# Weight sums of a block product made in DRAM by accumulating transfers, and one down projection moved to block products

## The chip, the cores and the metric

The kernel runs on one core of a Trainium2 chip. TensorE (PE) multiplies, VectorE (DVE), ScalarE (ACT) and GpSimd (POOL) work elementwise, SyncE (SP) only issues transfers. Each engine has its own instruction stream and works through it in order; engines wait for one another by semaphores. Transfers that SP issues are seen in the profile under SPq; POOL can issue transfers too.

The metric is the device time in microseconds of one execution. Three runs of the kernel before took 2127.66, 2130.86 and 2133.08 us.

## The reference

One decoder layer on 2048 tokens of width 1024, all in float32:

```python
xn = rms_norm(h, mix_norm_w)
proj = xn @ w_in                                   # 1024 x 3072
q, f_logit, i_v, g, lru_x, lru_gate = split(proj)
mixed = concat([hgrn2_mix(q, f_logit, i_v, g), rglru_mix(lru_x, lru_gate)])
h = h + mixed @ w_out                              # 1024 x 1024
hn = rms_norm(h, ffn_norm_w)
gate, up = split(hn @ w_gate_up)                   # 1024 x 5632, 2816 each
h = h + (silu(gate) * up) @ w_down                 # 2816 x 1024
return rms_norm(h, final_norm_w)
```

`hgrn2_mix` is a gated linear recurrence over 4 heads, `rglru_mix` a short convolution with a gated scan over 512 channels.

## The kernel before

**Halves.** The 2048 tokens are worked in two halves of 1024. The program runs the mixers of the first half, the mixers of the second, then the FFN (gate/up, then down) of the first half, then the FFN of the second.

**Precision.** A float32 operand is split into a high part, rounded for the fast matmul, and a low part, the rest (`split`: a cast on ACT at L207 and a subtraction on DVE at L208, for the mixers' weights L163 and L164). A product is three matmuls: high by high, high by low, low by high.

**Mixers.** A loop over eight strips of features and two chunks of 512 tokens (`s`, `c`), 16 turns for each half, multiplies the normalized input with `w_in` (L234 to L236) and runs the two recurrences on ACT and DVE. The weights come as a stream `ws` of 512 KB pieces (SP, L161) into three raw buffers. POOL does three small things a turn: `hist` (L389) keeps the end of a chunk for the convolution, `hst` (L427) the end of a scan, and `oss` (L379) takes the power -1/2 of a head's mean square, which DVE's L380 then multiplies with.

**Gate/up.** The products of the FFN are made in blocks of 2 x 2 by seven products instead of eight (Winograd's form of Strassen's method). A "quad" is one such block product: 22 for each half, 44 in all, each of 7 products of 12 matmuls (4 slices of the depth, 3 matmuls each, L614). It needs seven weight operands: three blocks as they are, and four sums s1 to s4 of blocks. `Sums.load` fetches two transfers of 512 KB a quad, `Sums.make` makes the sums on DVE (L498, tile `s`) and splits each operand (tiles `wgu`). Four PSUM banks a quad (`quad_a`, `quad_e`, `quad_f`, `quad_g`) take the products; ACT copies two of them out (`e`, L651 and L654), DVE adds the others (`u`, `e`).

**Down.** `store` writes the gated activations: for the column pairs worked in blocks their seven operands (`ao_p`, float32), for the others as they are. `Group` is a set of up to four of the 11 pairs of columns: its four weight blocks are loaded (`wdax`, `wdbx`, `wday`, `wdby`), the sums are made from them on DVE, and seven products follow (`down_quads`, L885: for four pairs 48 matmuls a product, for three pairs 36). The second half uses three groups: 4, 4 and 3 pairs. The first half uses two groups of 4 pairs in blocks; its last three pairs, six columns, are multiplied plainly by `down_plain` (L752 to L754, 48 matmuls a column, 24 for each of the two chunks). `residual_load`, `square` and `finish` add the residual stream, take the squares and write the output.

**Order.** The program is written with `bops`, `later`, `extra` and `steps`, lists of small pieces of work that the loops hand out one at a time; on top of that, a scheduler decides the order of the instructions on each engine. Buffers come from pools with a fixed number of slots (16 of 128 x 512 in "pg", 9 for split weights in "w"); a load waits until its slot is free. SP and POOL work through their queues in order, and each of them waits for an earlier transfer when it comes to the ninth outstanding one.

Of the kernel before, what the change touches and what calls it, by code (L numbers as in the profile page):

```python
# [13 lines left out]
P = 128  # L14
# [21 lines left out]
def hybrid_layer(ctx: ExitStack, tc: tile.TileContext, x, x_t, norm_w, cols, w_in, gate_w, w_out, w_gu, w_down, out):  # L36
# [117 lines left out]
    class Stream:  # L154
# [3 lines left out]
        def emit(self, i):  # L158
            src, nm = self.specs[i]
            raw = rawt("raw_" + nm)  # L160
            nc.sync.dma_start(out=raw, in_=src)  # L161
            hi, lo = wslot("whi_" + nm), wslot("wlo_" + nm)
            nc.scalar.copy(out=hi, in_=raw)  # L163
            v.tensor_tensor(out=lo, in0=raw, in1=f(hi), op=ALU.subtract)  # L164
            self.made[i] = (hi, lo)
# [338 lines left out]
    def acts(src, nm, direct):  # L504
        ops = {}
        held = []

        def put(name, k, p):
            split([ops[name][s][:, k, :] for s in range(2)], p)

        pages = {}

        def open_(names):
            for name in names:
                ops[name] = [block(f"act_{LET[name]}{s}_{nm}") for s in range(2)]


        def early(k):
            if k == 0:
                open_(("p1", "p5"))  # L520
            b11, b12 = (xin(f"{t}{k}_{nm}") for t in ("b11e_", "b12e_"))
            for p, c in ((b11, 0), (b12, 1)):
                nc.sync.dma_start(out=p, in_=src[0][k, :, c * CW : (c + 1) * CW])
            put("p1", k, b11)
            tt_(b12, b12, b11, SUB_)
            put("p5", k, b12)

        def load(k):
            if k == 0:
                open_(("p1", "p5", "p6", "p7", "p2", "p3", "p4") if direct else ("p6", "p7", "p2"))  # L530
            b11, b12 = (xin(f"{t}{k}_{nm}") for t in ("b11_", "b12_"))
            b21, b22 = ((late if direct else page)(f"{t}{k}_{nm}") for t in ("b21_", "b22_"))
            for p, n, c in ((b11, 0, 0), (b12, 0, 1), (b22, 1, 1), (b21, 1, 0)):
                nc.sync.dma_start(out=p, in_=src[n][k, :, c * CW : (c + 1) * CW])
            pages[k] = b11, b12, b21, b22

        def one(k):
            b11, b12, b21, b22 = pages[k]
            if direct:
                put("p1", k, b11)  # L540
            tt_(b11, b12, b11, SUB_)
            if direct:
                put("p5", k, b11)

        def two(k):
            b11, b12, b21, b22 = pages[k]
            tt_(b11, b22, b11, SUB_)
            tt_(b12, b22, b12, SUB_)
            put("p2", k, b21)
            put("p6", k, b11)  # L550
            tt_(b21, b21, b11, SUB_)
            put("p7", k, b12)
            if direct:
                put("p3", k, b22)
                put("p4", k, b21)
            held.append((b22, b21))

        def rest(i):
            name = ("p3", "p4")[i]
            ops[name] = [block(f"act_{LET[name]}{s}_{nm}") for s in range(2)]  # L560
            for k in range(4):
                put(name, k, held[k][i])
# [5 lines left out]
        if direct:  # L568
            return ops, steps, []
        return ops, [[lambda k=k: early(k) for k in range(4)], steps], [lambda: rest(0), lambda: rest(1)]  # L570

    ORDER = ("p1", "p5", "p6", "p7", "p2", "p3", "p4")


    class Sums:
        def __init__(self, src, nm):
            self.src, self.nm, self.op, self.raw, self.done = src, nm, {}, [None, None], set()

        def load(self, i):
            r = rawt(f"raw{i}_{self.nm}", (P, 2, CW))  # L580
            nc.sync.dma_start(out=r, in_=self.src[:, :, i * CW : (i + 1) * CW].rearrange("u p k -> p u k"))
            self.raw[i] = r

        def make(self, i):
            (a11, a21), (a12, a22) = ([r[:, u, :] for u in range(2)] if r is not None else (None, None) for r in self.raw)
            nm, name = self.nm, ORDER[i]
            if name == "p1":
                x = a11
            elif name == "p5":
                self.s1 = x = late("s1" + nm)  # L590
                tt_(x, a21, a22, ADD)
            elif name == "p6":
                self.s2 = x = late("s2" + nm)
                tt_(x, self.s1, a11, SUB_)
            elif name == "p7":
                x = late("s3" + nm)
                tt_(x, a11, a21, SUB_)
            elif name == "p2":
                x = a12
            elif name == "p3":  # L600
                x = late("s4" + nm)
                tt_(x, a12, self.s2, SUB_)
            else:
                x = a22
            w = wslot(f"wgu_{LET[name]}_{nm}", (P, 2, CW))
            split([w[:, s, :] for s in range(2)], x)
            self.op[name] = w

    def product(ps, w, b, first):
        for k in range(4):  # L610
            ks = slice(k * P, (k + 1) * P)
            hi, lo = b[0][:, k, :], b[1][:, k, :]
            for n, (s, x) in enumerate(((0, hi), (1, hi), (0, lo))):
                nc.tensor.matmul(  # L614
                    ps, lhsT=w[:, s, ks], rhs=x, start=first and k + n == 0, stop=k == 3 and n == 2, skip_group_check=not first
# [6 lines left out]
    def sums(q):  # L622
        if q < len(quads) and q not in made:
            half, j, m = quads[q]
            f0 = m * NF + 2 * j
            made[q] = Sums(w_gu[f0 : f0 + 2], f"{half}_{j}_{m}")
        return made.get(q)

    def sums_start(q):
        s = sums(q)  # L630
        s.load(0)
        s.load(1)

    def ffn_up(half, bops, between=()):
        between = list(between)
        q0 = half * 2 * NPAIR
# [535 lines left out]
```

## Time and profile before

| | |
|---|---|
| median of three runs | 2130.86 us (2127.66 to 2133.08) |
| the profiled execution, first to last instruction | 2131.1 us |
| the same by the list of cores, with the granted TensorE clock | 2131.1 us, 0.997 |
| PE busy | 2101.2 us, 99% |
| DVE busy | 1493.1 us, 70% |
| ACT busy | 1010.2 us, 47% |
| POOL busy | 82.2 us, 4% |
| transfers, mean over the span | 123 GB/s |
| first mixers' loop, first to last matmul of its kind | 62.6 to 291.3 us |
| gate/up of the first half begins | 849.5 us |
| last matmul of the plain columns | 1494.9 us |
| last matmul of the second half's gate/up | 1914.0 us |

The profiled execution is first to last instruction 0.2 us above the median of the runs, so a difference worked out on the trace is used on the median as it is. In the profile a line such as `L614 PE MATMUL quad_a<-act_a,wgu_a 128*128 128x512 f32 x528 | 127.5, 389 | 0.0` gives the line of the program, the engine and operation, output and inputs, shape, count, busy microseconds, mean nanoseconds of one, and the idle time ahead. Matmuls overlap one another, so 389 ns is how long one lasts and not how far apart they come: 528 of them are busy 127.5 us.

### The profile page before, as it was taken

What the parts mean: (1) busy time and instruction counts of PE and PEld (TensorE: products, weight loads), DVE (VectorE), ACT (ScalarE), POOL (GpSimd) and SP (SyncE); (2) the same over time, 40 slices, a digit from 0 to 9 for tenths busy, and PEclk for the clock granted to TensorE, in tenths of its full rate; (3) what the DMA queues carried; (4) which work ended last, traced back from release to release, by engine and by line L of the source; (5) the groups of instructions that cost most, each with busy time, mean ns of one, the idle gap of its engine ahead of it and who ended that gap; (6) DMA issues with size and microseconds to landing.
All of it is one profiled execution on the core that took longest, in us unless ns stands there. A gap on an engine that the chain in (4) does not pass through costs nothing.

```text
span 2131.1 us, 26161 instructions
## 1 busy us (share of the span) xinstructions
PE 2101.2 (99%) x9704; PEld 1735.7 (81%) x9704; DVE 1493.1 (70%) x2415; ACT 1010.2 (47%) x1647; POOL 82.2 (4%) x130
## 2 busy tenths in 40 slices
PE   8999999999999999999999999999999999999998
PEld 6887888888878888788888888888888888888887
DVE  6577664645776566877667669878867667669787
ACT  5577764535777644533333334335433333334333
POOL 2000001100000000000000000000000000000000
PEclk9999999999999999999999999999999999999999
DMA  6111104852111058433323257346423223257424
GB/s 216 61 40 40 40 20 160 282 162 69 31 39 40 20 174 260 156 112 99 106 93 129 89 187 253 109 136 205 143 94 119 95 90 123 94 206 252 156 88 143
DMA packets 138420, 262.84 MB, mean 123 GB/s; under 512 B 11186, under 2 KB 27570, under 8 KB 138292
## 3 DMA queue, kind: packets, MB, share of 16 engines
q1 hardware_dynamic: 138292, 261.17, 36.5%
q8 instruction: 76, 1.25, 0.2%
q14 instruction: 52, 0.43, 0.1%
HBM read 197.95 MB, written 63.18 MB: 123 GB/s over the span
## 4 chain that ended last, share of the span: by engine, by line
PE 83%; ACT 6%; DVE 5%; DMA 3%; issue 2%; SPq 0%; POOL 0%; DVEq 0%; POOLq 0%; ACTq 0%
PE quad_e L614 11%; PE quad_g L614 11%; PE quad_a L614 11%; PE pda L885 10%; PE pdb L885 6%; PE quad_f L614 5%; PE poh L246 2%; PE poh L247 2%; PE poh L248 2%; PE pb L236 2%; PE pb L234 2%; PE pb L235 2%; PE pa L234 1%; PE pa L235 1%; PE pg L248 1%
## 5 line engine op out<-in xcount | busy, mean ns | idle before, releaser
L614 PE MATMUL quad_f<-act_f,wgu_f 128*128 128x512 f32 x528 | 127.4, 389 | 1.8 <-DVE h L1050 1.7
L614 PE MATMUL quad_a<-act_a,wgu_a 128*128 128x512 f32 x528 | 127.5, 389 | 0.0
L614 PE MATMUL quad_g<-act_d,wgu_d 128*128 128x512 f32 x528 | 127.0, 389 | 0.2 <-DVE u L498 0.2
L614 PE MATMUL quad_g<-act_g,wgu_g 128*128 128x512 f32 x528 | 127.1, 390 | 0.0
L614 PE MATMUL quad_a<-act_b,wgu_b 128*128 128x512 f32 x528 | 127.1, 389 | 0.0
L614 PE MATMUL quad_e<-act_e,wgu_e 128*128 128x512 f32 x528 | 127.0, 389 | 0.0
L614 PE MATMUL quad_e<-act_c,wgu_c 128*128 128x512 f32 x528 | 126.9, 389 | 0.0
L614 PEld LDWEIGHTS quad_f<-act_f,wgu_f 128*128 128x128 f32 x528 | 99.0, 188 | 23.1 <-ACT act_g L207 2.1
L498 DVE TENSOR_TENSOR u<-u,quad_g 128x512 f32<-128x512 f32 x88 | 60.5, 687 | 80.9 <-PE quad_g L614 80.9
L614 PEld LDWEIGHTS quad_g<-act_d,wgu_d 128*128 128x128 f32 x528 | 99.0, 188 | 21.1 <-DVE u L498 0.6
L614 PEld LDWEIGHTS quad_e<-act_c,wgu_c 128*128 128x128 f32 x528 | 99.1, 188 | 20.6
L614 PEld LDWEIGHTS quad_g<-act_g,wgu_g 128*128 128x128 f32 x528 | 99.0, 188 | 20.8 <-DVE wgu_g L208 0.3
L614 PEld LDWEIGHTS quad_e<-act_e,wgu_e 128*128 128x128 f32 x528 | 99.0, 188 | 20.6
L614 PEld LDWEIGHTS quad_a<-act_b,wgu_b 128*128 128x128 f32 x528 | 99.0, 188 | 20.5
L614 PEld LDWEIGHTS quad_a<-act_a,wgu_a 128*128 128x128 f32 x528 | 98.9, 188 | 20.6 <-ACT act_c L207 0.2
L234 PE MATMUL pa<-xn,whi_in 128*128 128x512 f32 x256 | 101.7, 397 | 0.0
L236 PE MATMUL pb<-xn,whi_in 128*128 128x512 f32 x256 | 101.0, 395 | 0.0
L235 PE MATMUL pb<-xn,wlo_in 128*128 128x512 f32 x256 | 101.0, 394 | 0.0
L234 PE MATMUL pb<-xn,whi_in 128*128 128x512 f32 x256 | 100.9, 394 | 0.0
L235 PE MATMUL pa<-xn,wlo_in 128*128 128x512 f32 x256 | 100.6, 393 | 0.0
L236 PE MATMUL pa<-xn,whi_in 128*128 128x512 f32 x256 | 100.5, 393 | 0.0
L248 PE MATMUL poh<-whi_o,mx 128*128 128x512 f32 x256 | 99.9, 391 | 0.0
(331 smaller groups left out, 4940.9 us busy)
## 6 DMA issues: line engine op xcount, KB each, us to landing
raw<-in_w_gu SPq DMA_DIRECT2D x88, 512.0 KB, 3.8
raw_in<-in_w_in SPq DMA_DIRECT2D x48, 512.0 KB, 3.5
ao_p<-as SPq DMA_DIRECT2D x76, 256.0 KB, 2.6
raw_o<-in_w_out SPq DMA_DIRECT2D x32, 512.0 KB, 4.4
x<-in_x SPq DMA_DIRECT2D x32, 256.0 KB, 5.8
xrh<-in_x SPq DMA_DIRECT2D x32, 256.0 KB, 3.9
h<-h SPq DMA_DIRECT2D x32, 256.0 KB, 3.5
hn<-hths SPq DMA_DIRECT2D x32, 256.0 KB, 3.3
```

Of the source, the lines that this page charges most:

```text
L234: nc.tensor.matmul(ps, lhsT=whi[:, ks], rhs=hi, start=(k == 0), stop=False)
L235: nc.tensor.matmul(ps, lhsT=wlo[:, ks], rhs=hi, start=False, stop=False)
L236: nc.tensor.matmul(ps, lhsT=whi[:, ks], rhs=lo, start=False, stop=(k == KT - 1))
L246: nc.tensor.matmul(ps, lhsT=hi, rhs=whi[:, ks], start=(k == 0), stop=False)
L247: nc.tensor.matmul(ps, lhsT=hi, rhs=wlo[:, ks], start=False, stop=False)
L248: nc.tensor.matmul(ps, lhsT=lo, rhs=whi[:, ks], start=False, stop=(k == KT - 1))
L498: (e or v).tensor_tensor(out=out, in0=a, in1=b, op=op)
L614: nc.tensor.matmul(ps, lhsT=w[:, s, ks], rhs=x, start=first and k + n == 0, stop=k == 3 and n == 2, skip_group_check=not first)
L885: nc.tensor.matmul(ps, lhsT=x, rhs=y, start=first and q + n == 0, stop=q == gr.n - 1 and n == 2, skip_group_check=not first)
```

## The change

It lays the FFN weights out in DRAM by quadrants, makes the four sums of both weight matrices in DRAM, and works all of the first half's down projection in blocks.

- **Sums in DRAM.** `combine` makes them for a piece of two quads (or two column pairs of `w_down`), 17 pieces in all: step 0 is four copies of 512 KB, DRAM to DRAM, issued by SP behind the latest weight load of the mixers; steps 1, 2 and 3 are two, one and one accumulating transfers issued by POOL, each adding a block, or a sum made before, onto a copy. `combines(t)` hands them out in the mixers' loop, a new piece every one and a half turns and a step of a piece every two turns. 11 pieces belong to gate/up, 6 to down.
- **Gate/up.** A quad loads its seven operands ready, as 256 KB each (`Sums.load`), and splits them two at a time (128 x 1024). The form of the method is another one: the signs differ, three banks a quad instead of four, products in the order p1, p5, p6, p3, p7, p2, p4, three copies out of PSUM on ACT, and fewer DVE operations.
- **Store.** For the last three column pairs of either half the seven operands are split already here (`keep_`) and written as high and low parts, 14 transfers instead of seven.
- **Down.** Both halves use the groups of 4, 4 and 3 pairs. A group loads its weight operands ready (`wr`, L810). The group of three loads its activation operands already split, straight into slots of the "w" pool (`aop`, L831). The second half's activation operands are made in pieces during the first half's down (`extra`), and the output of the first half's first four tiles is written during the second half's gate/up.

```diff
-            nc.sync.dma_start(out=raw, in_=src)
+            self.last = nc.sync.dma_start(out=raw, in_=src)
...
+    def combine(w, sums_, p, step):
+        s1, s2, s3, s4 = (sums_[i][p] for i in range(4))
+        n = s1.shape[0]
+        a11, a12, a21, a22 = (w[i, p * PIECE : p * PIECE + n] for i in range(4))
+        if step == 0:
+            with tc.issue_after(ws.last.ins):
+                for s, a in ((s1, a21), (s3, a11), (s2, a11), (s4, a12)):
+                    nc.sync.dma_start(out=s, in_=a)
+        else:
+            for s, a in (((s1, a22), (s3, a21)), ((s2, s1),), ((s4, s2),))[step - 1]:
+                nc.gpsimd.dma_start(out=s, in_=a, accum_op=ADD, max_dma_last_dim=8192)
+
+    def combines(t):
+        for i, piece in enumerate(pieces):
+            step, odd = divmod(t - 3 * i // 2, 2)
+            if not odd and 0 <= step < 4:
+                combine(*piece, step)
...
         def load(self, i):
+            names = ORDER[2 * i : 2 * i + 2]
             r = rawt(f"raw{i}_{self.nm}", (P, 2, CW))
-            nc.sync.dma_start(out=r, in_=self.src[:, :, i * CW : (i + 1) * CW].rearrange("u p k -> p u k"))
+            for u, name in enumerate(names):
+                nc.sync.dma_start(out=r[:, u, :], in_=summed(w_gu, gu_s, name, self.q, 1)[0])
...
         def make(self, i):
-            elif name == "p5":
-                self.s1 = x = late("s1" + nm)
-                tt_(x, a21, a22, ADD)
-            elif name == "p6":
-                self.s2 = x = late("s2" + nm)
-                tt_(x, self.s1, a11, SUB_)
...
+            hi, lo = (wslot(f"wgu{'hl'[z]}{i}_{self.nm}", (P, 2, CW)) for z in range(2))
+            split((hi[:, 0:n, :], lo[:, 0:n, :]), self.raw.pop(i)[:, 0:n, :])
...
-            b1, b3, b2, b4 = (mk(f"quad_{i}_{nm}") for i in "aefg")
-            dst = dict(p1=b1, p5=b3, p6=b2, p7=b4, p2=b1, p3=b3, p4=b4)
+            ba, bb, bc_ = (mk(f"quad_{i}_{nm}") for i in "abc")
+            dst = dict(p1=ba, p5=bb, p6=ba, p3=bb, p7=ba, p2=bc_, p4=ba)
...
+        def keep_(name, p):
+            hl = [sb.tile([P, CW], F32R, tag="late", name=f"ah{z}_{name}_{half}_{j}", bufs=5) for z in range(2)]
+            split(hl, p, -1.0 if name == "p6" else None)
+            for z in range(2):
+                nc.sync.dma_start(out=as_d[half][name][z][j - SPLIT], in_=f(hl[z]))
...
         def fetch(self, i):
             name = DORDER[i]
+            t = block(f"wr_{LET[name]}_{self.nm}", F32)
+            for k, m in self.parts():
+                nc.sync.dma_start(out=t[:, k : k + m, :], in_=summed(w_down, dn_s, name, self.j0 + k, m).rearrange("g p t -> p g t"))
+            self.wraw[i] = t
+            if self.split:
+                return
...
         def make(self, i, part):
+                if self.split:
+                    for (k, m), t in zip(self.parts(), self.a[name]):
+                        j = self.j0 - SPLIT + k
+                        for z in range(2):
+                            nc.sync.dma_start(out=f(t[z])[:, 0:m, :], in_=as_d[self.half][name][z][j : j + m].rearrange("g p t -> p g t"))
...
+                combines(half * 16 + s * NC + c)
...
     for half in range(2):
-        ffn_up(half, bops[half], later if half == 0 else ())
-        hp = residual(half)
+        ffn_up(half, bops[half], later)
+        hp, later = residual(half), []
...
-            down_quads(0, ((0, 4), (4, 4)), hp, False)
-            bops[1], steps, last = acts(hn_d[1], "1", True)
...
-            for c in range(NC):
-                down_plain(0, c, range(16, NF), hp, extra, [lambda i=i: first(i) for i in range(7)] if c == 1 else ())
...
-            down_quads(1, ((0, 4), (4, 4), (8, 3)), hp, True)
+        down_quads(half, hp, extra, later)
```

In the rows below the line numbers of the program after are its own; a product of the block method that is L614 before is L636 after, and L885 is L875.

POOL in the first mixers' loop, from the first head's `oss` on. Before:

```order
L379 TENSOR_TENSOR oss_0_0_936<-oss_0_0_936,tinies 128x4
L389 COPY hist<-xp_1_1_1109 128x3
L379 TENSOR_TENSOR oss_0_1_1052<-oss_0_1_1052,tinies 128x4
L427 COPY hst<-t_1_0_1071 128x1
L427 COPY hst<-t_1_1_1171 128x1
L389 COPY hist<-xp_3_0_1485 128x3
L379 TENSOR_TENSOR oss_2_0_1418<-oss_2_0_1418,tinies 128x4
```

The same place after (`gus` are the gate/up sums; 8 and 10 are two pieces):

```order
L379 TENSOR_TENSOR oss_0_0_1028<-oss_0_0_1028,tinies 128x4
L596 DMA gus_6_114<-gus_6_103 64x2048
L596 DMA gus_6_136<-gus_6_114 64x2048
L389 COPY hist<-xp_1_1_1203 128x3
L379 TENSOR_TENSOR oss_0_1_1146<-oss_0_1_1146,tinies 128x4
L596 DMA gus_8_104<-in_w_gu 64x2048
L596 DMA gus_8_126<-in_w_gu 64x2048
L596 DMA gus_10_105<-in_w_gu 64x2048
L596 DMA gus_10_127<-in_w_gu 64x2048
L427 COPY hst<-t_1_0_1165 128x1
L596 DMA gus_8_115<-gus_8_104 64x2048
L596 DMA gus_10_116<-gus_10_105 64x2048
```

POOL's small operations now stand behind accumulating transfers, of which one that reads a sum (`gus_6_136<-gus_6_114`) follows the one that makes it.

SP in the same loop, after; before, the four weight loads stand there with nothing between them:

```order
L161 DMA raw_in_12_1480<-in_w_in 128x1024
L161 DMA raw_in_13_1486<-in_w_in 128x1024
L593 DMA gus_8_104<-in_w_gu 16x8192
L593 DMA gus_8_126<-in_w_gu 16x8192
L593 DMA gus_8_115<-in_w_gu 16x8192
L593 DMA gus_8_137<-in_w_gu 16x8192
L593 DMA gus_10_105<-in_w_gu 16x8192
L593 DMA gus_10_127<-in_w_gu 16x8192
L593 DMA gus_10_116<-in_w_gu 16x8192
L593 DMA gus_10_138<-in_w_gu 16x8192
L161 DMA raw_in_14_1727<-in_w_in 128x1024
L161 DMA raw_in_15_1733<-in_w_in 128x1024
```

Eight copies of 512 KB now lie between one pair of weight loads and the next.

SP in the group of three of the first half's down, after:

```order
L810 DMA wr_f_8_11826<-dns_8_154 128x2x512
L810 DMA wr_f_8_11826<-dns_10_155 128x512
L831 DMA aop_f_0_8_11864<-as_p_222 128x2x512
L831 DMA aop_f_0_8_11865<-as_p_223 128x2x512
L831 DMA aop_f_0_8_11866<-as_p_222 128x512
L831 DMA aop_f_0_8_11867<-as_p_223 128x512
L810 DMA wr_e_8_11889<-dns_8_148 128x2x512
L810 DMA wr_e_8_11889<-dns_10_149 128x512
```

Each product of that group has its weight operand fetched in two transfers and its split activation operand in four; before, this part of the program was plain columns with a load of 512 KB of weights and 256 KB of activations each.

More of the change, by code (lines that the diff above doesn't have):

```diff
@@ L524, in early @@
             put("p1", k, b11)
-            tt_(b12, b12, b11, SUB_)
+            tt_(b12, b11, b12, SUB_)
             put("p5", k, b12)
         def load(k):
[L529 to L534, printed above, removed]
@@ L564, in acts, with four @@
+        def four(f_):
+            return [lambda k=k: f_(k) for k in range(4)]
         steps = [lambda: load(0)]
@@ L567, in acts, with sum_tiles @@
             steps.append(lambda k=k: two(k))
[L568 to L572, printed above, removed]
+        return ops, [four(early), steps], [lambda: rest(0), lambda: rest(1)], [four(f_) for f_ in (early, mid, third, fourth, fifth)]
+    ORDER = ("p1", "p5", "p6", "p3", "p7", "p2", "p4")
+    PIECE = 2
+    NQ = 2 * NPAIR
+    def sum_tiles(n, nm):
+        return [
+            [dram.tile([min(PIECE, n - p), P, CW], F32, name=f"{nm}{i}_{p}") for p in range(0, n, PIECE)] for i in range(4)
+        ]
@@ L630, in sums_start @@
         s = sums(q)
-        s.load(0)
-        s.load(1)
+        for i in range(3):
+            s.load(i)
     def ffn_up(half, bops, between=()):
-        between = list(between)
-        q0 = half * 2 * NPAIR
-        for q in range(q0, q0 + 2 * NPAIR):
+        between, chores = list(between), []
+        q0 = half * NQ
+        for q in range(q0, q0 + NQ):
             _, j, m = quads[q]
             nm = f"{half}_{j}_{m}"
-            s, nxt, nn = sums(q), sums(q + 1), sums(q + 2)
+            s, nxt = sums(q), sums(q + 1)
@@ L691, in ffn_up @@
-                if nxt is not None and not end:
-                    nxt.make(i)
-                    nxt.done.add(i)
+                        sg21 = page("sg21" + nm)
+                        nc.scalar.activation(out=sg21, in_=ba, func=AF.Silu, scale=-1.0)
+                    else:
+                        v.scalar_tensor_tensor(out=sg21, in0=ba, scalar=-1.0, in1=sg21, op0=MUL, op1=MUL)
+                        chores = store(half, j, a11, a21, sg21, a22)
+                ahead(s, nxt, i, end)
@@ L859, in down_quads @@
         u2 = {}
-        groups[0].load()
         fetch(0)
@@ L898, in down_quads @@
                     tt_(h00, h00, ps, ADD)
-                    if end and last:
+                    if end:
                         square(half, tt, 0, h00)
```

367 lines of the change are left out of this document (165 added, 202 removed).

## Prediction

> **What bounds the kernel now.** I read the list of cores first (2131.1 us, clock 0.997: nothing throttled), then the page's engine line, then windows of the stages.
>
> ```profile
> core 0: 2131.1 us, clock 0.997
> PE 2101.2 (99%) x9704; PEld 1735.7 (81%) x9704; DVE 1493.1 (70%) x2415; ACT 1010.2 (47%) x1647; POOL 82.2 (4%) x130
> ```
>
> TensorE is idle for 30 us of the whole span. The windows say where (columns: stretch, its length, busy time and count of PE, weight loads, DVE, ACT, POOL, then clock, share of the DMA engines, GB/s):
>
> ```profile
> 160.00:213.00 53.00, 50.13 (x245) 41.45 (x244) 37.93 (x88) 40.86 (x66) 3.93 (x6) 0.97 0.12 40
> 852.00:905.00 53.00, 50.52 (x232) 40.02 (x231) 46.42 (x79) 31.31 (x65) 3.94 (x4) 1.00 0.47 154
> 905.00:1280.00 375.00, 375.00 (x1656) 310.52 (x1655) 256.03 (x379) 131.53 (x216) 0.00 (x0) 1.00 0.34 118
> 1276.00:1300.00 24.00, 24.00 (x108) 19.87 (x107) 24.00 (x23) 12.66 (x15) 0.00 (x0) 1.00 1.03 369
> 1500.00:1914.00 414.00, 414.00 (x1828) 342.80 (x1827) 289.68 (x434) 145.64 (x241) 1.74 (x2) 1.00 0.35 119
> 2090.00:2131.00 41.00, 33.61 (x149) 27.50 (x147) 32.51 (x56) 12.40 (x29) 4.84 (x8) 0.95 0.45 154
> ```
>
> From 905 us on PE is busy 375 of 375 and 414 of 414 us in the two gate/up stretches, and 24 of 24 even where DVE and the DMA engines are full. What is idle lies in the mixers (2.9 us in the stretch shown), at the start of gate/up (2.5 us) and at the tail (7.4 us). So in the FFN only the number of matmuls can shorten the time, as long as what feeds them stays ahead. The chain of waits gives the spacing of the matmuls:
>
> ```profile
> PE 83%; ACT 6%; DVE 5%; DMA 3%; issue 2%; SPq 0%; POOL 0%; DVEq 0%; POOLq 0%; ACTq 0%
> 1935.93 10.88 PE pdb L885 x48
> ```
>
> 10.88 / 48 = 0.2267 us for each.
>
> **Removed: 36 matmuls.** The plain columns are 288 matmuls on the path:
>
> ```profile
> L752 PE MATMUL pd<-whi_d,ad 128*128 128x512 f32 x96 | 36.6, 391 | 0.7 <-DVE hd L498 0.7
> L753 PE MATMUL pd<-wlo_d,ad 128*128 128x512 f32 x96 | 37.4, 389 | 0.0
> L754 PE MATMUL pd<-whi_d,ad 128*128 128x512 f32 x96 | 37.4, 389 | 0.0
> L885 PE MATMUL pda<-wd_a,aop_a 128*128 128x512 f32 x228 | 53.1, 389 | 0.0
> ```
>
> The 228 of a product are 4 groups of 48 and one of 36; the new group of three adds 36 to each of seven products, 252. All other matmuls stay. 288 x 0.2267 = 65.3 us become 252 x 0.2267 = 57.1 us: **-8.2 us**. The plain stage's wait of 0.7 us for `hd` goes with it: **-0.7 us**.
>
> **Removed: DVE work, worth nothing.** A quad made four sums, in groups such as
>
> ```profile
> L498 DVE TENSOR_TENSOR s<-raw,s 128x512 f32<-128x512 f32 x44 | 30.4, 691 | 1.2
> L164 DVE TENSOR_TENSOR wlo_in<-raw_in,whi_in 128x1024 fp32r<-128x1024 f32 x48 | 58.6, 1220 | 22.0 <-PE pv L248 7.1 <-PE pb L235 6.3 <-ACT whi_in L163 5.0
> ```
>
> 4 x 0.69 = 2.8 us a quad on DVE, about 120 us in 44 quads; splits of 128 x 1024 at 1.22 us instead of two at 0.69 save a little more. PE covers it all: DVE was busy 256 of 375 us and PE never idle. I book 0; the 2.5 us at the start of gate/up, where DVE is busiest, is the most that could come back.
>
> **Moved: banks in gate/up.** Three banks a quad are handed on more often. In the new order of the matmuls at least 22 lie between a bank's last matmul and its next writer: 22 x 0.2267 = 5.0 us. Within these ACT copies the bank out, in the worst case behind a cast:
>
> ```profile
> L651 ACT COPY e<-quad_a 128x512 f32<-128x512 f32 x44 | 25.8, 587 | 66.3 <-PE quad_a L614 66.3
> L163 ACT CAST whi_in<-raw_in 128x1024 fp32r<-128x1024 f32 x48 | 50.3, 1047 | 18.8 <-DMA raw_in<-in_w_in 17.4 <-PE pv L248 1.1
> ```
>
> 0.59 + 1.05 = 1.6 us, with a Silu of about the copy's length 2.3 us. Hidden: 0. If that cover failed, each us would cost 44 us over the quads. Gate/up loads 7 x 256 KB a quad instead of 2 x 512 KB: 0.79 MB more in 84 x 0.2267 = 19.0 us, 41 GB/s on top of 118, of 369 that the stretch at 1276 moved. 0.
>
> **Added: the group of three in the first half.** A product there is 36 x 0.2267 = 8.2 us. For each, SP brings the activation operand already split, 2 x 3 x 256 KB = 1.57 MB, and the weight operand, 0.79 MB. The nearest rows:
>
> ```profile
> ra_a<-ao_p SPq DMA_DIRECT2D x9, 512.0 KB, 3.6
> wdax<-in_w_down SPq DMA_DIRECT2D x4, 1024.0 KB, 5.5
> wdby<-in_w_down SPq DMA_DIRECT2D x4, 1024.0 KB, 12.1
> ```
>
> At 369 GB/s the 2.36 MB take 6.4 us; a load of 512 KB alone takes 3.6, of which 1.4 is transfer, so 2.2 us are fixed: 8.6 us, 0.4 late a product if both come in one product's time, 3.1 us over seven. If the weights were fetched earlier, 4.3 + 2.2 = 6.5 us, and nothing is late. I take the middle: **+1.5 us**. Bounds: 0 below; above, 12.1 us (the fourth of four loads in a row) for each, 3.9 late x 7 = 27 us. The second half's group had its loads before too, so there only the 0.79 MB more count: inside the same bounds.
>
> **Added: transfers in the mixers.** The first half's loop ran at 40 GB/s from 62.6 to 291.3 us, 229 us for 16 turns, 14.3 us each. Into it come 44 copies and 44 accumulates of 524 KB (11 pieces, one per 21.4 us). With 17 weight loads, 8.9 MB, and every transfer counted once: 55 MB / 369 = 149 us of 229. Copies ahead of a weight load delay it: eight copies of one issue are 4.2 MB, 11.4 us (23 if both sides count). The lead of the weights:
>
> ```profile
> 108.97 0.33 SPq L161 DMA_DIRECT2D raw_in<-in_w_in  x1
> 143.50 1.04 ACT L163 CAST whi_in<-raw_in 128x1024 fp32r<-128x1024 f32 x1
> ```
>
> With three raw buffers this load is cast 34.5 us later. 11 to 23 us on top of 3.5 is hidden.
>
> *The accumulates.* No row shows one. Below, a plain load of 512 KB alone (3.6 us); above, 12.1 us in a queue; I take 5.5, one load of twice the bytes, since an accumulate reads two streams. By that row nothing queues and the sum stays at 2124.
>
> A rule speaks against it. The Trainium skill, "Collectives: The Full Stack", section "The bandwidth ceiling: the fold count and why AG ≠ RS ≠ AR", says that an adding transfer puts two source reads for one write on the same ring and so ran at about half a copy's rate. By it (an estimate) the loop would hold 78 MB, 212 us of its 229, transfers would queue, and the time would be that of the first rival below, 2141 or more. No row of this case shows it, and the page's setting is a ring of several ranks, not one queue.
>
> *POOL.* An accumulate that reads a sum waits on POOL for the one that made it, and `oss` waits behind it. The tight places:
>
> ```profile
> 102.04 1.04 POOL L379 TENSOR_TENSOR oss<-oss,tinies 128x4 f32<-128x4 f32 x1 [7.31 <-DVE oss L378]
> 113.64 1.01 POOL L379 TENSOR_TENSOR oss<-oss,tinies 128x4 f32<-128x4 f32 x1 [4.70 <-DVE oss L378]
> 126.03 0.71 POOL L427 COPY hst<-t 128x1 f32<-128x1 f32 x1 [11.37 <-DVE t L426]
> 144.62 2.37 POOL L427 COPY hst<-t 128x1 f32<-128x1 f32 x1 [17.89 <-DVE t L426]
>   DVE v L380: 1.4, 2
> ```
>
> Between the first two `oss`, 11.6 us apart, the new order puts the third and fourth sum of a piece, that is two chained waits: 5.8 us for each before `oss` is late. What follows is DVE's L380 (the last row: the only one that ever waited for `oss`), and behind it all of DVE, which is idle 53 - 37.93 = 15.1 of 53 us, 4 us a turn. The copies of `hst` have 18 us before the next scan needs them. At 5.5 us nothing is late: 0. It is the thinnest margin of the sum.
>
> **Sum:** 2131.1 - 8.2 - 0.7 + 1.5 = 2123.7 us; the profiled execution is 0.2 us over the median, so 2124 us.
>
> **Rivals.**
>
> 1. *POOL held by slow accumulates* (slower). At 12.1 us each, two chained waits are 24.2 us in a gap of 11.6: 12.6 us late, less the 4 us of slack, 8.6. With one such place for each of the 16 `oss`, fewer in the second half (6 of 17 pieces), half of them tight: 4 x 8.6 = 34 in the first and about 2 x 8.6 = 17 in the second, 2174; with two places only, 2141. It decides from 5.8 + 4/2 = 7.8 us an accumulate on. For it: no row shows accumulates cheap, copies and weights share the engines. Against: the engines stood at a share of 0.12 there.
>
> 2. *The gain is spent on late operands* (no change). The group of three waits longer, or the first quads do, which take sums and split operands from new places: 1 us late a product and 2 or 3 us at the two starts of gate/up give back 7 + 3 of 8.9: 2131 (2125 to 2137). For it: `wdby` at 12.1 us when several loads come together. Against: PE stayed full at 369 GB/s.
>
> 3. *Bank hand-offs* (slower). If one in each quad were late by 0.5 us, 22 us: 2144. Against: 5.0 us of cover for 2.3 us of work; ACT idle half the time.
>
> 4. *The change shortens a stage that nobody ends on.* If the second half's gate/up had to wait for its activation operands, the last of which are now made in the last product of the first half's down, the 8.2 us would be waited there instead: 2131. For it: in that product 8 splits and 4 subtractions of 128 x 512 fall together, 12 x 0.69 = 8.3 us of DVE in a product of 8.2. Against: the operands of gate/up's first four products are made 9 to 16 products earlier, and their 48 matmuls, 10.9 us, cover the rest.
>
> **How the numbers follow.** A measurement of this kernel tells about 0.3% (6.4 us) from no change: faster is below 2124.5, slower above 2137.3. The forecast gets 0.55 and a range of its own from 2119 (no operand late, the 2.5 us at the start of gate/up gone: 2131.1 - 8.9 - 2.5 = 2119.7) to 2129 (a product 0.9 us late); 0.45 of it faster, 0.10 the same. Rival 1 gets 0.20, 0.17 slower; rival 2 0.17, 0.14 the same and 0.03 slower; rival 3 0.05, slower; rival 4 0.03, the same. Faster 0.45, the same 0.10 + 0.03 + 0.14 + 0.03 = 0.30, slower 0.25. For 8 in 10 the range takes in rival 2 and the near end of rival 1: 2118 to 2141.
>
> **What would show it.** Right: no L752; seven groups of the down matmuls with 264 each at 0.227 us spacing; PE full in both gate/up stretches with DVE near 60%; waits of PE in the group of three of some tenths of a us; waits on `oss` no longer than now; accumulates that land within 8 us. Wrong: PE waiting for L380's successors or for `whi_in` in the first mixers' loop (rival 1), for `aop` in the group of three (rival 2), for ACT's copies in each quad (rival 3). The forecast fails if the loop before 291 us grows by more than 5 us.

## The result, and the profile after

The changed kernel takes **2191.65 us** (2190.83 to 2194.23 in four runs) against 2131.30 us before: a ratio of 1.0286, 95% interval 1.0272 to 1.0301. It is 60 us slower; 2124 us was forecast, and the range ended at 2141.

The list of cores and the page's engine line of the changed kernel:

```profile
core 0: 2190.4 us, clock 0.985
PE 2108.6 (96%) x9668; PEld 1737.0 (79%) x9668; DVE 1288.6 (59%) x2053; ACT 1015.8 (46%) x1578; POOL 131.7 (6%) x198
PE 74%; DMA 11%; ACT 7%; DVE 5%; issue 2%; SPq 1%; POOL 0%; DVEq 0%; ACTq 0%; POOLq 0%
```

The count is as forecast, 36 matmuls fewer, but PE is idle for 82 us instead of 30, and it is busy 7.4 us longer on fewer matmuls: the granted clock is 0.985 instead of 0.997. In the chain of waits (last line) transfers hold 11% instead of 3%. The first and last matmuls of the stages say where the time went; the four columns add up to the span:

| | gate/up begins | first half: gate/up and down | second half | tail | span |
|---|---|---|---|---|---|
| before | 849.5 | 645.4 | 628.3 | 7.9 | 2131.1 |
| after | 878.3 | 650.1 | 652.0 | 10.0 | 2190.4 |
| difference | +28.8 | +4.7 | +23.7 | +2.1 | +59.3 |

The first half grows by only 4.7 us because its 36 matmuls fewer hide part of what it lost.

What PE waited for, in the two kernels' lists of waits (us in total, times, longest). Before:

```profile
PE pk L329 <- DVE lg L315: 6.5, 3, 2.9
```

After:

```profile
PE pda L875 <- ACT u L884: 20.6, 2, 10.7
PE pk L329 <- DVE lg L315: 20.0, 6, 8.7
PE pr L411 <- ACT xh L207: 4.4, 1, 4.4
PE pi L411 <- DVE v L380: 4.3, 1, 4.3
...
PE quad_a L636 <- DVE wgul L208: 2.8, 4, 0.7
PE quad_a L636 <- DVE e L498: 2.3, 1, 2.3
PE quad_a L636 <- ACT e L672: 1.3, 2, 1.1
```

Two places stand out: the mixers (L329, L411), and one wait of some 10 us at the start of each down (L875 on ACT's copy `u`). A third, at the start of the second half's gate/up, is seen only once the wait on `u` is gone (first experiment).

**The mixers.** Windows of PE alone over the first mixers' loop (length, busy time, clock, share of the transfer engines, GB/s). Before:

```profile
53.00:320.00 267.00, 261.04 (x1339) 0.99 0.12 41
```

After:

```profile
53.00:320.00 267.00, 244.95 (x1232) 0.96 0.80 212
```

The share went from 0.12 to 0.80, and from 53 to 160 us the engines were full (1.03 and 1.02). The loop's last product with `w_in` starts at 314.1 us instead of 291.1. Two things came late behind the full engines. The first is a weight load, seen in the chain of waits and on ACT; the second is POOL's `oss`, held behind an accumulate:

```profile
59.92 24.70 DMA raw_in<-in_w_in
...
174.83 5.15 DMA gus<-gus
...
246.37 11.29 DMA gus<-gus
257.66 0.35 issue
258.01 1.59 POOL gus L596 x2
259.60 1.08 POOL oss L379
```

```profile
84.64 1.05 ACT L163 CAST whi_in<-raw_in 128x1024 fp32r<-128x1024 f32 x1 [15.46 <-DMA raw_in<-in_w_in]
```

A load that landed in 3.5 us before takes 24.7 here and holds ACT for 15.5. The line of the accumulates (L596) and the line of `oss` (L379) in the changed kernel:

```profile
DMA to landing us min/median/max: 3.8/12.2/21.0
```

```profile
  DVE v L380: 21.5, 7
```

An accumulate takes 12.2 us in the median. The fastest one of 512 KB took 5.1 (in the chain above); the 3.8 is one of 256 KB, in the last piece. DVE waited 21.5 us for `oss`, 1.4 before.

**The start of a down.** The timeline of ACT, then of PE, in the first half:

```profile
1334.82 0.61 ACT L207 CAST ah_p<-as 128x512 fp32r<-128x512 f32 x1
1337.81 0.59 ACT L884 COPY u<-pda 128x512 f32<-128x512 f32 x1 [2.38 <-DMA as_p<-ah_p]
1339.10 0.59 ACT L884 COPY u<-pda 128x512 f32<-128x512 f32 x1 [0.70 <-DMA as_p<-ah_p]
1340.98 0.59 ACT L884 COPY u<-pda 128x512 f32<-128x512 f32 x1 [1.29 <-DMA as_p<-ah_p]
```

```profile
1325.74 1.97 PE L875 MATMUL pdb<-wd_f,aop_f 128*128 128x512 f32 x8
1338.45 10.34 PE L875 MATMUL pda<-wd_b,aop_b 128*128 128x512 f32 x36 [10.73 <-ACT u L884]
```

`u` takes the first product out of its PSUM banks, so that the second can have them. It needs a slot of the pool `late`, five slots of 128 x 512, and `keep_` of the change puts its split operands (`ah`) into the same five. Each copy of `u` waits for a store of `as_p` to land and give a slot back.

### The profile page after: what moved, and what is told of

Read it like the earlier page. It is cut to its first block, busy times and chain, and to the rows that moved or that the text cites. A ratio compares the mean times of both kernels' runs of the same rounds, so it can differ in the third digit from the quotient of the medians.

```text
span 2190.4 us, 26588 instructions
## 1 busy us (share of the span) xinstructions
PE 2108.6 (96%) x9668; PEld 1737.0 (79%) x9668; DVE 1288.6 (59%) x2053; ACT 1015.8 (46%) x1578; POOL 131.7 (6%) x198
## 4 chain that ended last, share of the span: by engine, by line
PE 74%; DMA 11%; ACT 7%; DVE 5%; issue 2%; SPq 1%; POOL 0%; DVEq 0%; ACTq 0%; POOLq 0%
PE quad_a L636 20%; PE pda L875 10%; PE quad_b L636 10%; PE pdb L875 7%; PE quad_c L636 5%; PE poh L246 3%; PE poh L248 3%; PE poh L247 3%; DMA raw_in<-in_w_in 3%; DMA gus<-in_w_gu 2%; DMA as_p<-ah_p 2%; PE pg L248 1%; PE pg L247 1%; PE pg L246 1%; DMA hd<-h 1%
## 5 line engine op out<-in xcount | busy, mean ns | idle before, releaser
L208 DVE TENSOR_TENSOR wgul<-raw,wguh 128x1024 fp32r<-128x1024 f32 (+1 forms) x176 | 191.5, 1088 | 257.3 <-issue 76.9
L207 ACT CAST wguh<-raw 128x1024 fp32r<-128x1024 f32 (+1 forms) x176 | 166.6, 947 | 339.4 <-PE quad_a L636 148.4
L636 PE MATMUL quad_a<-act_a,wguh 128*128 128x512 f32 x352 | 118.4, 389 | 0.9 <-ACT wguh L207 0.9
L636 PE MATMUL quad_a<-act_d,wguh 128*128 128x512 f32 x352 | 116.4, 391 | 2.3 <-DVE e L498 2.3
L636 PE MATMUL quad_b<-act_e,wguh 128*128 128x512 f32 x352 | 117.8, 389 | 0.0
L636 PE MATMUL quad_c<-act_b,wguh 128*128 128x512 f32 x352 | 116.9, 393 | 0.6 <-ACT wguh L207 0.6
L636 PE MATMUL quad_a<-act_f,wguh 128*128 128x512 f32 x352 | 115.9, 390 | 1.3 <-ACT e L672 1.3
L636 PE MATMUL quad_a<-act_g,wguh 128*128 128x512 f32 x352 | 115.5, 389 | 0.0
L636 PE MATMUL quad_b<-act_c,wguh 128*128 128x512 f32 x352 | 115.5, 389 | 0.0
L247 PE MATMUL poh<-wlo_o,mx 128*128 128x512 f32 x256 | 99.9, 393 | 0.0
L875 PE MATMUL pda<-wd_b,aop_b 128*128 128x512 f32 x264 | 65.1, 405 | 20.6 <-ACT u L884 20.6
L636 PEld LDWEIGHTS quad_a<-act_d,wguh 128*128 128x128 f32 x352 | 66.3, 188 | 16.4 <-DVE e L498 2.6
L636 PEld LDWEIGHTS quad_c<-act_b,wguh 128*128 128x128 f32 x352 | 67.1, 191 | 15.0 <-ACT wguh L207 1.0
```

The source lines that it names most:

```text
L207: nc.scalar.copy(out=dst[0], in_=src)
L208: v.tensor_tensor(out=dst[1], in0=src, in1=f(dst[0]), op=ALU.subtract)
L247: nc.tensor.matmul(ps, lhsT=hi, rhs=wlo[:, ks], start=False, stop=False)
L636: nc.tensor.matmul(ps, lhsT=w[s][:, ks], rhs=x, start=first and k + n == 0, stop=k == 3 and n == 2, skip_group_check=not first)
L875: nc.tensor.matmul(ps, lhsT=x, rhs=y, start=first and q + n == 0, stop=q == gr.n - 1 and n == 2, skip_group_check=not first)
```

## The experiments

Each kernel is the changed one unless another is named. Stage times are in the table behind the last experiment.

**Whole stores.** `SPLIT = NPAIR`: nothing is split before it is stored.

```diff
-    SPLIT = 8
+    SPLIT = NPAIR
```

> The changed kernel, but the operands of the last three column pairs are stored whole and split in the down projection, as for the other pairs; no split store. Theory A (the two waits of 10.7 and 9.9 us at the start of each down, where PE waits for ACT's copy of u, come from u sharing the five slots of the late pool with the split stores): both waits go, and the slower matmuls after them, 2 x 2 us, so 2191.7 - 20.6 - 4 = 2167 us, 2162 to 2172. Rival B (ACT is late there because its casts wait for the down's first loads): the waits stay, 2186 to 2193.

Measured: 2175.7 us, 1.0205 (1.0188 to 1.0222) of before; 16 us faster than the changed kernel. Both waits on `u` are gone, so theory A has the cause in the split stores. The run takes out their casts on ACT too, so it does not separate the slots from these; that the slots held the copies is read from the timeline above. The time is 9 us over the one that theory A gave, and 3.7 over its range: a new wait is now seen at the start of the second gate/up, which is not in the changed kernel's list (PE waits of this run):

```profile
PE quad_a L636 <- ACT act_d L207: 7.8, 3, 5.0
PE quad_c L636 <- ACT wguh L207: 3.0, 1, 3.0
```

**No sums in DRAM.**

```diff
-                combine(*piece, step)
+                pass
...
-        return sums_[{"p5": 0, "p6": 1, "p7": 2, "p3": 3}[name]][j // PIECE][j % PIECE : j % PIECE + n]
+        return w[{"p5": 2, "p6": 0, "p7": 3, "p3": 1}[name], j : j + n]
```

> The changed kernel without any sums in DRAM: no copies and no accumulating transfers, and the operands that should be sums are read from single blocks of the weights, so the sums are left out of what is computed. Theory A (the copies and accumulates cost the mixers 23 us in the first half and 6 in the second): gate/up begins at about 850 us instead of 878 and the time is 2191.7 - 29 = 2163 us, 2158 to 2167. Rival B (something else in the mixers moved too, such as the order of their instructions): gate/up still begins after 860, over 2173 us.

Measured: 2161.36 us, 1.0142 (1.0127 to 1.0157); 30.3 us faster, and gate/up begins at 846.4. Theory A: the sums, and nothing else in the mixers, cost the 29 us.

**Copies without additions.**

```diff
-            if not odd and 0 <= step < 4:
+            if not odd and step == 0:
```

> The changed kernel with step 0 alone: the copies are made, the additions onto them are left out. Theory A (POOL's small operations are held behind waits for accumulates, and the accumulates take most of the engines' time): the first mixers' loop loses 5 to 10 us instead of 23, the rest being weight loads behind copies; 2172 to 2179 us. Rival B (the weight loads behind the copies are all of it): the loop still loses over 18 us, 2185 to 2192. Rival C (the additions are all of it): the loop loses under 3 us, 2163 to 2168.

Measured: 2163.85 us, 1.0153 (1.0138 to 1.0168), gate/up at 848.1. Rival C: the copies with their place ahead of the weight loads cost 2.5 us, the additions 27.8. The share of the engines in the first loop:

```profile
53.00:320.00 267.00, 260.66 (x1343) 1.00 0.36 126
```

44 copies are worth 0.24 of 267 us, 1.46 us of all engines each; the 44 accumulates on top 0.44, 2.67 us each.

**`oss` off POOL.** DVE's reciprocal in place of POOL's power.

```diff
-        nc.gpsimd.tensor_tensor(out=ss, in0=ss, in1=mhalf, op=ALU.pow)
+        v.reciprocal(out=ss, in_=ss)
```

> The changed kernel with the one tight operation taken off POOL: DVE takes the reciprocal of oss in place of POOL's power -1/2, so the square root is left out of what is computed there; copies and accumulates stay. Theory A (holding oss on POOL costs about half of the mixers' 29 us): 2175 to 2182 us, and no wait on DVE's L380 any more. Rival B (full transfer engines that make the weights late are the cause, POOL only shows it): 2187 to 2192.

Measured: 2182.43 us, 1.0241 (1.0226 to 1.0256): 9.2 us faster, gate/up at 869.8. It lies 0.4 us above the range of theory A: holding `oss` on POOL is about 9 of the 29 us. The greater part stays, and with it the late weights. ACT's waits for them in the changed kernel, then in this run (17.4 us before):

```profile
ACT whi_in L163 <- DMA raw_in<-in_w_in: 47.2, 10, 15.5
```

```profile
ACT whi_in L163 <- DMA raw_in<-in_w_in: 48.7, 9, 17.0
```

**Plain copies on POOL.** The accumulates without the addition, in the same order with the same waits.

```diff
-                nc.gpsimd.dma_start(out=s, in_=a, accum_op=ADD, max_dma_last_dim=8192)
+                nc.gpsimd.dma_start(out=s, in_=a, max_dma_last_dim=8192)
```

> The changed kernel with POOL's transfers as plain copies instead of additions, in the same order with the same waits; the additions are left out. Theory A (an accumulate costs about 1.84 copies because it reads two streams: 0.44 of 267 us for 44 of them against 0.24 for 44 copies): the engines' share in the first loop falls from 0.80 to about 0.60, and the time to 2168 to 2179. Rival B (transfers that POOL issues are dear in themselves): the share stays over 0.75 and the time at 2186 to 2193.

Measured: 2171.15 us, 1.0189 (1.0173 to 1.0204), gate/up at 855.2.

```profile
53.00:320.00 267.00, 256.37 (x1302) 0.99 0.61 211
```

Theory A: (0.61 - 0.36) x 267 / 44 = 1.52 us of all engines for a copy that POOL issues, as much as one by SP; adding makes it 2.67, 1.8 times. The chained waits on POOL are all still here, but shorter, since one of these copies lands in 7.9 us in the median: DVE waits 2.7 us for `oss` instead of 21.5, ACT 35.6 us for weights instead of 47.2, and gate/up begins 6 us later than before instead of 29. So the engine time of the additions lies behind both losses in the mixers; this run does not tell the two apart, the one before does. ACT's waits for weights are not all passed on to PE, as the 35.6 us show. Whether the second read or the adding itself makes an accumulate dear is not shown by a run. The Trainium skill ("Collectives: The Full Stack", section "The bandwidth ceiling: the fold count and why AG ≠ RS ≠ AR") puts it down to the two reads, with a factor of 1.93 in its setting; here it is 1.8, and the prediction's estimate by that rule, 212 us of engine time for the loop, stands against 0.80 x 267 = 214.

**Sums spread out.** With whole stores, one gate/up piece every three turns instead of one and a half, the down's pieces in the first half's gate/up.

```diff
-            step, odd = divmod(t - 3 * i // 2, 2)
-            if not odd and 0 <= step < 4:
+            step = t - 3 * i
+            if 0 <= step < 4:
                 combine(*piece, step)
...
+            if half == 0:
+                downs(q)
```

> The changed kernel with whole stores (as the run before with that edit, 2175.7 us) and the sums spread out: one gate/up piece every three turns over both halves' mixers, one step a turn, the down's pieces in the first half's gate/up. Theory A (the accumulates hurt because they fill the transfer engines): in the first loop 6 pieces instead of 11 take the engines' share from 0.80 to about 0.5, the two loops lose under 6 us of the 30, 2147 to 2158 us. Rival B (chained waits on POOL hold oss whatever the load): the loops still lose over 12 us, 2158 to 2170.

Measured: 2212.79 us, 1.0391 (1.0373 to 1.0408). The time is far outside both theories, but the mixers show theory A: share 0.50, gate/up begins at 851.9. The 11 pieces that are left in the mixers cost 2.4 us, all 17 in a burst 28.8, though DVE still waits 11.0 us for `oss`.

```profile
53.00:320.00 267.00, 261.75 (x1337) 0.99 0.50 135
...
850.00:1280.00 430.00, 374.33 (x1611) 0.94 0.59 180
```

The loss moved: the scheduler put all of the down's copies and accumulates around the start of gate/up (POOL issued them from 841.6 to 935.0 us), where the engines were full for 100 us and PE idle for half of it, since nothing in the program held them back.

**The down alone.** Mixers, gate/up and its sums as in the kernel before; only the first half's down in blocks, its sums made in DRAM during gate/up.

```diff
-            down_quads(0, ((0, 4), (4, 4)), hp, False)
...
-            for c in range(NC):
-                down_plain(0, c, range(16, NF), hp, extra, [lambda i=i: first(i) for i in range(7)] if c == 1 else ())
+        down_quads(half, hp, extra, later)
...
+            if half == 0:
+                downs(q)
```

`down_quads` has three groups in both halves here, and `downs` in `ffn_up` makes the down's sums.

> The down part of the change with the kernel before elsewhere: gate/up sums on DVE, four banks a quad, as before; nothing added to the mixers; operands stored whole; all of the first half's down in blocks, its weight sums made in DRAM (24 copies, 24 accumulates) while the first half's gate/up runs. Theory A (the 36 matmuls are worth their 8.2 us, and all that was lost came from the transfers in the mixers, the slots of the split store and the new gate/up): 2131.3 - 8.9 = 2122, 2119 to 2127 us. Rival B (the start of a down, or of the second gate/up, where operands and residual come together, waits by itself): 2129 to 2140.

Measured: 2202.52 us, 1.0333 (1.0318 to 1.0349). The whole time says little, for the reason of the run before: without a weight load to stand behind, the copies went to the very start of the program, which had a share of 0.99 there, and gate/up began at 909.6. The stage itself is as forecast: the first half's gate/up and down take 637.3 us instead of 645.4, **8.1 less**. But the second half takes 640.9 instead of 628.3, 12.6 more, with a wait at its start:

```profile
PE quad_e L676 <- ACT wgu_e L207: 7.4, 1, 7.4
```

With the tail, 2.0 longer, the stages add up to 2131.1 - 8.1 + 12.6 + 2.0 = 2137.6 us: with the late start of gate/up left out, this run bears out rival B.

**Whole stores and no sums.** The first two edits together.

```diff
-                combine(*piece, step)
+                pass
...
-    SPLIT = 8
+    SPLIT = NPAIR
```

> Whole stores and no sums at all in DRAM (operands that should be sums are single blocks; the sums are left out of what is computed). If the two losses are separate they add: 2191.7 - 30.3 - 16.0 = 2145, 2142 to 2149 us, and the 14 us over 2131 that stay lie in the FFN, in waits at the start of the second gate/up. If they share a cause, above 2150.

Measured: 2143.06 us, 1.0061 (1.0046 to 1.0076). The two losses add. The first half takes 638.7 us, 6.7 less than before; the second takes 645.9, 17.6 more, and that lies in its first 50 us: 147 matmuls instead of 227.

**p4's operand from p6's.** On top of that, `fifth`, which loads four blocks again for each slice of p4's operand, is left out; the operand comes from parts already there.

```diff
+            tt_(t, f(ops["p6"][0][:, k, :]), f(ops["p6"][1][:, k, :]), ADD)
+            tt_(b21, b21, t, ADD)
+            put("p4", k, b21, -1.0)
```

> Whole stores, no sums (2143.1 us; the sums are left out of what is computed), and the last operand of the second gate/up made from parts that are on the chip: p4's is p6's high plus low part and the block that p2 loads anyway, so 16 loads and 8 DVE operations fewer at the start of the second gate/up. Theory A (these loads, spread over 25 us by the four input slots, hold PE there): 2131 to 2138 us. Rival B (the start is bound by ACT and DVE, which also finish the output there): 2140 to 2145.

Measured: 2133.78 us, 1.0012 (1.0003 to 1.0021): 9.3 us faster. Theory A: the late making of that operand held PE. The edit takes out 16 loads and four DVE operations (not eight: 2035 against 2039), and moves the operand from the first quads into the down; which of these did it was not separated.

**The whole change, paced.** Whole stores, sums spread, the down's copies behind gate/up's weight loads (`tc.issue_after`), p4 from p6; nothing left out.

```diff
-            with tc.issue_after(ws.last.ins):
+            with tc.issue_after((Sums.last if w is w_down else ws.last).ins):
```

> The whole change with correct sums and three edits: whole stores, the gate/up sums spread over both halves' mixers and the down's sums paced by the first gate/up's weight loads, p4's operand made from p6's. Theory A (the sums are free when the transfer engines stay under about 0.6): 2 to 5 us over the run without sums and with the same p4 edit, 2133 to 2143. Rival B (accumulates delay the weight loads of gate/up, which have one quad of lead): 2146 or more.

Measured: 2141.16 us, 1.0055 (1.0039 to 1.0070): 50 us of the 60 are back, and all sums are made in DRAM. Gate/up begins at 850.9. It is 7.4 us over the run without sums, a little more than the 2 to 5 given.

**The down alone, paced.** The same pacing and p4 edit on the kernel with the down part only, and the first quad's weights loaded two products earlier.

```diff
+            with tc.issue_after(Sums.last.ins):
+                for s, a in ((s1, a21), (s3, a11), (s2, a11), (s4, a12)):
+                    nc.sync.dma_start(out=s, in_=a)
...
-            extra[20, 0] = [lambda: sums_start(q), third[0], third[1]]
+            extra[18, 0] = [lambda: sums_start(q)]
```

> The down part alone again (gate/up, its sums and the mixers as before), with the down's sums paced by the first gate/up's weight loads, p4's operand made from p6's, and the first weights of the second gate/up loaded two products earlier into a free large slot. Theory A (with nothing late at the start of the second gate/up the 36 matmuls are worth their 8.9 us): 2121 to 2127 us. Rival B (the start still waits for ACT and DVE): 2129 to 2137.

Measured: 2138.79 us, 1.0041 (1.0029 to 1.0054): far from theory A, and 1.8 us beyond the range of rival B. The first half is 4.7 us shorter than before, the second 9.7 longer. PE waits at the switch to the second gate/up, then ACT's cast behind the first of them, which itself waited for the sum `s`:

```profile
PE quad_e L680 <- ACT wgu_e L207: 4.5, 1, 4.5
PE quad_f L680 <- ACT wgu_f L207: 1.8, 1, 1.8
```

```profile
1495.84 0.62 ACT L207 CAST wgu_e<-s 128x512 fp32r<-128x512 f32 x1 [1.04 <-DVE s L498]
```

**Three operands not made.** To see whether the operand work holds that switch:

```diff
+            for name in ("p2", "p3", "p4"):
+                bops[1][name] = bops[1]["p1"]
```

> The down part alone and paced (2138.8 us), with three of the second gate/up's seven activation operands (p2, p3, p4) not made: their products read p1's operand, so the second half's gate/up is not what the reference computes, while every matmul stays. Theory A (what keeps the 36 matmuls' 8.2 us from showing is the operand work pressed into the switch from the first half's down to the second gate/up, where 11 us are lost): 2138.8 - 11 = 2128, 2125 to 2131 us, and no wait over 1 us on PE there. Rival B (the switch is held by the weights' sums and the output's last scaling, not by the operands): 2134 to 2139.

Measured: 2140.44 us, 1.0029 (1.0016 to 1.0041): not faster, 1.4 us beyond the range of rival B. Theory A fell: with the work gone, the wait on `wgu_e` is 7.2 us. DVE's timeline shows what is ahead of the sum `s` that `wgu_e` is cast from:

```profile
1487.76 4.07 DVE L829 SCALAR_TENSOR_TENSOR hd<-hd,sf,wfin 128x512 f32<-128x512 f32 x6 [0.41 <-POOL sf L824]
...
1495.33 2.48 DVE L498 TENSOR_TENSOR hd<-hd,pdb 128x512 f32<-128x512 f32 x4
1497.72 0.69 DVE L498 TENSOR_TENSOR s<-rawq 128x512 f32<-128x512 f32 x1
```

The weights `rawq` had been asked for at 1466, by this run's group of that tile; the first sum comes 31 us later, behind the output's scaling (L829) and the down's last additions (L498). The cast of `wgu_e` follows at 1502.2, 3.8 us after that sum, behind ACT's casts of `wd_b` and some squares.

**Weight sums ahead.** The first three sums of that quad are made during the last two products of the down. In the same edit the output norm's weights move out of the slots for split weights.

```diff
+            extra[19, 1] = [lambda: sums(q).one()]
+            extra[19, 2] = [lambda: sums(q).two()]
+            extra[19, 3] = [lambda: sums(q).three(), lambda: first(0), lambda: first(1)]
```

> The down part alone and paced (2138.8 us), with the first three weight sums of the second gate/up's first quad made during the last two products of the first half's down, ahead of the down's last additions on DVE, and the output norm's weights in a raw slot instead of a slot for split weights. Theory A (PE waits 4.5 and 1.8 us at the switch, and runs slowly after it, because these sums stand behind the down's last additions on DVE): 2126 to 2132 us, waits of PE at the switch under 2 us. Rival B (the switch is held by something else, the slots or ACT): 2135 to 2140.

Measured: 2133.47 us, 1.0007 (0.9998 to 1.0016): no difference from before that can be measured, and between the ranges of the two theories. Of the waits on `wgu_e` and `wgu_f` 0.3 us are left. So the order on DVE was their cause, unless the freed slot had a part in it, which this run does not separate; the cast shown in the down alone, paced, waited for the sum. 5.3 us of the time are back. Waits on other operands of the first quads are left:

```profile
PE quad_f L696 <- ACT wgu_c L207: 2.3, 1, 2.3
PE quad_a L696 <- ACT wgu_a L207: 1.0, 2, 0.8
```

The stages of the runs that the argument rests on, from the first and last matmul of each:

| | gate/up begins | first half | second half | tail | span |
|---|---|---|---|---|---|
| before | 849.5 | 645.4 | 628.3 | 7.9 | 2131.1 |
| after | 878.3 | 650.1 | 652.0 | 10.0 | 2190.4 |
| whole stores | 877.1 | 639.3 | 647.5 | 10.1 | 2174.0 |
| no sums | 846.4 | 651.6 | 651.2 | 9.7 | 2158.9 |
| whole stores, no sums | 850.6 | 638.7 | 645.9 | 9.8 | 2145.0 |
| the same, p4 from p6 | 849.2 | 640.0 | 634.6 | 9.8 | 2133.6 |
| whole change, paced | 850.9 | 642.9 | 634.1 | 10.1 | 2138.0 |
| down alone, paced | 848.2 | 640.7 | 638.0 | 9.8 | 2136.7 |
| the same, sums ahead | 851.7 | 639.3 | 634.3 | 9.0 | 2134.3 |

Taken out one after the other, the sums gave 30.3 us (2191.65 to 2161.36), the split stores 18.3 (to 2143.06) and the late operand of p4 9.3 (to 2133.78): 57.9 of the 60 us. No version was faster than the kernel before.

## Why the prediction was wrong

- **36 matmuls, -8.2 us: right.** 9668 matmuls ran instead of 9704. The first half's FFN is 8.1 us shorter with the down alone, and 2.5 to 6.7 us shorter in the other runs without split stores (the one with the sums spread out aside), where PE waits more for operands. The further -0.7 for the wait on `hd` was wrong: the group of three has the same wait (0.7 us in the run with whole stores and no sums).
- **DVE's sums worth nothing: right.** PE was full before, and DVE's 200 us less bought nothing, but for the 2.5 us at the first start of gate/up, which the prediction kept as a bound: the stretch from 880 to 933, the same place after, is 53.00 of 53.00 busy.
- **Banks handed on behind 5.0 us of matmuls: right for the first half.** In the 375 us from 905 on PE was busy 372.2, and its waits there were for split weights (2.8 us), not for banks. In the second half's gate/up it did wait 3.6 us for banks to be emptied (`quad_a` on the two `e` in its list of waits).
- **The group of three, +1.5 us: nearer 0, and a cost left out.** Its loads landed in 3.8 to 5.0 us, and no wait of PE lies in it in the changed kernel. But the step stopped at the loads. The stores of the same operands were described ahead of the prediction and never costed: 14 transfers a pair through `ah` slots shared with `u`. That is 20.6 us of waits, 16 us net in the run with whole stores. It was in neither the sum nor a rival.
- **"By that row nothing queues", 0 for the transfers in the mixers: the step that failed first.** The term was put at 0 and cost 29 us. The 5.5 us for an accumulate are near the fastest one, 5.1, but in the median they took 12.2. The prediction counted each transfer once, 149 of 229 us; the engines' time was 1.8 times a copy's for each accumulate, and the engines were full for 107 us of the loop. The rule that spoke against it was quoted and set aside for coming from another setting; the trace gave its number.
- **Weights hidden by 34.5 us of lead: wrong at the place that mattered.** The row quoted is from the middle of the loop. The load issued at 59.92 us would have been wanted at 69.2, when ACT began to wait for it: 9 us of lead, with eight copies just ahead of it.
- **Rival 1 (POOL held): near, and mis-sized.** Its mechanism is there, DVE's waits for `oss` rose from 1.4 to 21.5 us, at 12.2 us an accumulate against the 12.1 of its bound. But taking `oss` off POOL gave 9 us only: the late weights behind full engines are left, and the greater part of the 29 us with them. Its upper case of 2174 is the nearest to the time measured, by luck: half of the 60 us came from places that it does not touch.
- **Rivals 2 and 4: near in part.** Nothing came late in the group of three, but the second gate/up does wait for operands made late, 9.3 us by p4's alone, in the first quads and not in the last product of the down. (The 7 + 3 us of rival 2 are more than the 8.9 that they are taken from; its time is 2132.)
- **The chances.** The cases were treated as one or the other; four losses came together, late weights, a held POOL, stores that held `u`, and late operands, and one of them stood in no case. A wait of 10 us costs more than it lasts, as the last section shows.

What is not settled: the second half that is 6 us longer in the last run, and the 1 to 2 us longer tail, which were seen and not taken apart; how far the late weights alone make up the 20 us that the mixers still lose without `oss` on POOL; and whether the slots alone, or ACT's casts too, made the wait on `u`.

## What to carry to other kernels

Work moved onto "idle" transfer engines has to be priced in engine time, with an accumulate as nearly two copies (1.8 here), and has to be paced by something that the program itself holds back; here all 17 pieces in a burst cost the mixers 29 us, 11 of them spread out 2.4, and with the other six paced too the sums cost 7.4 us in all. Before a new buffer goes into a shared pool, list what else takes a slot there, and when that slot comes free: a slot that is freed by a store is freed when the store lands. And where PE is full, what a change saves in one stage shows only if the next stage's first operands are ready that much earlier; look at the switch between stages first.

## What the runs showed of the hardware

TensorE's clock fell during a wait and stayed low after it. Windows of 1 us around the wait of 10.73 us in the changed kernel (busy time and count of PE, then the granted clock, share and GB/s):

```profile
1331.00:1332.00 1.00, 0.00 (x0) 1.00 1.04 383
1332.00:1333.00 1.00, 0.00 (x0) 0.64 1.05 401
1333.00:1334.00 1.00, 0.00 (x0) 0.50 1.05 404
...
1341.00:1342.00 1.00, 1.00 (x3) 0.50 1.05 393
1342.00:1343.00 1.00, 1.00 (x5) 0.74 1.05 385
1343.00:1344.00 1.00, 1.00 (x6) 1.00 1.05 389
```

PE stopped at 1327.7 us; by the window with 0.64 the clock fell to 0.50 about 4.6 us later, and by the one with 0.74 it came back about 4.1 us after work began again at 1338.45. The 36 matmuls behind the wait took 10.34 us instead of 8.2, so this wait cost about 2 us on top of its length. The changed kernel's matmuls were busy 7.4 us longer although 36 fewer, 15.6 us in all. The clock records of the two traces give 13.0 of these to the clock: PE was busy for 35.7 us at half clock, against 9.7 before. The Trainium skill ("TensorE: Matmul & The Clock Gate", Part 1) describes such a gate: half the clock until PE has been busy for about 3.4 us, and in its example half the clock again 5.2 us after the last matmul. The trace is near both, with 4.1 and 4.6 us.

An accumulate also costs POOL more to issue than a plain copy: 0.78 us against 0.50 in the run with plain copies.
